# Row groups of 1, 3, 4 and 8 row tiles instead of 4, 6 and 6, and another order of the opening

## The chip, the cores and the metric

The kernel runs on one core of one Trainium2 chip. The metric is the device time of one execution in microseconds. Before the change the median of three runs was 1383.23 us (1383.08 to 1383.5). The profile is of one further execution.

## The reference, cut to what matters

One decoder block works on 256 rows `x` of width 2048 and on one conditioning vector `c`. What the change touches is its first part:

```
c_act = silu(c)
mod = c_act @ w_ada + b_ada              # 6 vectors of 2048
sh1, sc1, g1, sh2, sc2, g2 = split(mod, 6)
h = rms_norm(x, norm_mix_g) * (1.0 + sc1) + sh1
proj = h @ w_in                          # 2048 -> 1024 u, 1024 q, 1024 k, 1024 v, 2048 ga, 2048 gb
```

After it come a state-space branch on `u`, attention on `q`, `k`, `v`, a gated merge of both, `w_out`, a second modulated norm, a squared-ReLU MLP and a final norm. Everything is float32.

## The kernel before, in words

**The product.** `h` is held transposed, in 16 row tiles of 128 of the 2048 inner rows (`ah` is its high part, `al` the rest). A weight tile is 128 rows by 1024 columns, 512 KB. SP's queue loads it into one of 7 `wraw` buffers (`load`, L156). ScalarE casts its high part into one of 4 `whi` buffers (L161), VectorE subtracts to give the low part, one of 4 `wlo` buffers (L163). TensorE then does three products for each output piece: high by high, high by low, low by high. `gemm_t` does that with 24 matmuls of 256 columns for a tile (L208 to L210), `gemm_n` with 12 of 512 columns (L261 to L265). `whi` and `wlo` of a tile are free when TensorE has done with it, `wraw` when the low part is made.

**Row groups.** Row tile k of `h` needs entries of `sc1` and `sh1` that come from `w_ada`, 2 MB for each row tile. So the products with `w_in` are not run column block after column block over all 16 row tiles. `GR` cuts the row tiles into groups, and `qkvu(which, g0, g1)` runs one column block (0 q, 1 k, 2 v, 3 u, 4 the first half of ga) over the groups g0 to g1. `evac` (L1066) copies the four PSUM banks of the sums to SBUF. A later group of the same block starts from these sums: `seeded` (L192) copies them back into PSUM, and the first matmul waits for that. There are 5 banks for this, so four of a new product come free only as the last one's are copied out.

**w_ada.** Row tiles 0 to 3 take theirs on TensorE (`ada_first`): `wan` loads of 512 KB, four for each row tile (L283), 32 matmuls against the conditioning vector (L295, tile `adap`), a copy (L299), and a column of sums (L305, tile `adac`) that becomes `A1` and `B1` (L970, L971, L976). Row tiles 4 to 15 take theirs on VectorE (`ada_wide`): two row tiles need four tiles `ahm` of 128 by 2048, each of two 512 KB loads (L361) and one multiply-and-sum with `cb`, the vector silu(c) spread over all partitions (L367). The `ahm` buffers are four at first and two from the 13th load on; a load goes out when the sum that frees its buffer is done. After the fourth sum ScalarE makes two row tiles of `h` (`make_h1`, L500 and L161), and VectorE their low part (L163).

**Order.** Queues of jobs ("lanes") are advanced once for each weight tile, so a rate decides after how many tiles a `w_ada` sum or a piece of the state-space set-up is put in. `want` pulls the `w_ada` jobs forward if a tile would need a row tile that isn't yet made. The scheduler then orders each engine's instructions, and each engine and SP's queue work in that order.

**The opening.** `x` comes in four loads. ScalarE squares each (L477), VectorE adds halves (L478), TensorE sums over partitions (L480, tile `ss`). VectorE and ScalarE turn that into `R`, one over the root mean square (L483 to L488), `scale1` multiplies `x` by it (L493), `make_h1` applies `A1` and `B1`. `ada_bcast` (L413, L414) spreads silu(c) with 16 broadcast matmuls. `ssm_params` puts some 90 small operations on VectorE. `idle` (L130) issues matmuls whose result nobody reads, eight for each of row tiles 1 to 3.

Of the kernel before, what the change touches and what calls it, by code (L numbers as in the profile page):

```python
# [19 lines left out]
P = 128  # L20
S = 256
# [35 lines left out]
GR = (4, 6, 6)  # L57
# [20 lines left out]
class Kern:  # L78
    def __init__(self, ctx, tc, a, out):
# [15 lines left out]
        self.want = lambda kt: None  # L95

# [91 lines left out]

    def seeded(self, banks, seed):
        for o, d in zip(banks, seed or ()):  # L190
            with self.tc.high_priority(offset=OFF):
                self.nc.scalar.copy(*d(o))  # L192
        return bool(seed)

    def gemm_t(self, src, kts, c0, xh, xl, koff=0, mid={}, homes=(), seed=None):
# [4 lines left out]
        for i, (kt, hi, lo) in enumerate(self.stream(src, kts, c0, homes)):  # L200
# [39 lines left out]
    def gemm_n(self, src, kts, c0, xh, xl, koff=0, tail=1, mid={}, homes=(), seed=None):  # L240
# [5 lines left out]
        for i, unit in enumerate(self.stream(src, kts, c0, homes)):  # L246
# [158 lines left out]
    def ada_bcast(self, cols, dst, gate=None, turn=True):  # L405
        p = self.aux("adab")
        for i in range(4):
            with self.after(gate):
                o, c = p[:, i * P:(i + 1) * P], cols[:, i:i + 1].to_broadcast([P, P])
                if turn:  # L410
                    self.nc.tensor.transpose(o, c, self.ident)
                else:
                    self.nc.tensor.matmul(o, c, self.ident, start=True, stop=True)  # L413
# [57 lines left out]
    def norm1(self):  # L471
# [4 lines left out]
        for i in range(4):  # L476
            nc.scalar.activation(jk[:, i], x[:, 4 * i:4 * i + 4, :], AF.Square)  # L477
            v.tensor_add(jk[:, i, 0:2], jk[:, i, 0:2], jk[:, i, 2:4])  # L478
            for k in range(2):
                nc.tensor.matmul(p[:, 0:S], self.ones, jk[:, i, k], start=i + k == 0, stop=i + k == 4)  # L480
# [3 lines left out]
        nc.scalar.activation(s, w, AF.Sqrt)  # L484
# [5 lines left out]
    def scale1(self, k0, gate=None, n=2):  # L490
        x = self.x[:, k0:k0 + n, :]
        with self.after(gate):
            self.nc.vector.tensor_mul(x, x, self.R[:, None, :].to_broadcast([P, n, S]))  # L493
# [443 lines left out]
    def body(self):  # L937
        nc, a, v = self.nc, self.a, self.nc.vector
        with self.hot():
# [7 lines left out]
            v.memset(self.eps, EPS)  # L947
            nc.scalar.activation(self.col("dum0", 1), self.eps, AF.Silu)
# [7 lines left out]
            self.ident = self.col("ident", P)  # L956
            make_identity(nc, self.ident)
# [16 lines left out]
        def fin_shift(vec, B, k0, n):  # L974
            s = slice(k0, k0 + n)
            return lambda acc: v.tensor_add(B[:, s], acc, self.bada[vec][:, s])  # L976
# [561 lines left out]
```

## Time and profile before

| | |
|---|---|
| median of 3 runs | 1383.23 us |
| the profiled execution's own time | 1383.14 us |
| its span, first to last instruction | 1381.3 us |
| outside the span | 1.84 us |
| mean granted clock of TensorE | 0.996 |
| TensorE busy | 1352.4 us, 98% |
| VectorE busy | 1043.7 us, 76% |
| ScalarE busy | 741.1 us, 54% |

Times in the views are microseconds from the first instruction. A busy TensorE is not TensorE at its full rate: matmuls overlap, and the profile models their ends. The distance from one start to the next tells the rate.

### The profile page before, as it was taken

The page shows a single profiled execution, that of the slowest core. Times are in us where ns is not written, and L with a number is a line of the kernel's source. Part 1 is how long each engine was busy: PE and PEld are TensorE (multiplying, and loading weights), DVE is VectorE, ACT ScalarE, POOL GpSimd, SP SyncE. Part 2 cuts the span into 40 slices and gives each one's busy share as a digit, 9 for nine tenths or more (in the row PEclk, how much of TensorE's full clock was granted, in tenths as well). Part 3 has the DMA queues.
Part 4 walks back from the last instruction along what each step waited for, and adds up shares of the span by engine and source line. Part 5 has one row for each costly group of instructions (what it writes and reads, how often), then busy time and mean ns, then how long its engine had stood idle before and what let it go on. Part 6 is the DMA issues. An engine that isn't in the chain of part 4 may idle for free.

```text
span 1381.3 us, 21633 instructions
## 1 busy us (share of the span) xinstructions
PE 1352.4 (98%) x8338; PEld 1173.9 (85%) x8338; DVE 1043.7 (76%) x1449; ACT 741.1 (54%) x1020; POOL 42.6 (3%) x96
## 2 busy tenths in 40 slices
PE   6999999999999999999999999999999999999997
PEld 5888899988888887888999888888888888888885
DVE  6699987687898898988886976777666555555676
ACT  4466658656557643446565655444453554634543
POOL 1000000500003000000000000000000000000000
PEclk9999999999999999999999999999999999999999
DMA  9999965898447889898697878788878656566561
GB/s 371 387 400 371 354 206 176 263 333 280 164 160 235 298 294 341 294 391 290 212 361 242 284 248 251 244 251 286 246 240 242 200 189 197 188 190 195 179 202 64
DMA packets 112423, 356.43 MB, mean 258 GB/s; under 512 B 12240, under 2 KB 12272, under 8 KB 111904
## 3 DMA queue, kind: packets, MB, share of 16 engines
q1 hardware_dynamic: 109280, 348.96, 74.5%
q0 software_dynamic: 2896, 5.83, 1.4%
q8 instruction: 65, 1.06, 0.3%
q10 hardware_dynamic: 144, 0.26, 0.1%
q14 instruction: 38, 0.31, 0.1%
HBM read 350.79 MB, written 2.51 MB: 256 GB/s over the span
## 4 chain that ended last, share of the span: by engine, by line
PE 59%; DVE 3%; DMA 1%; ACT 1%; issue 1%; DVEq 0%; ACTq 0%
PE pd L226 13%; PE pn L261 11%; PE pn L263 11%; PE pn L265 11%; PE pd L230 7%; PE pt L208 2%; PE pt L210 2%; PE pt L209 2%; DVE wraw L325 1%; DMA wraw<-in_w_proj_ssm_dram 1%; DVE wlo L163 1%; DMA wraw<-in_w_out_dram 0%; DMA wraw<-in_w_ff_dram 0%; ACT whi L161 0%; PE trm L1232 0%
## 5 line engine op out<-in xcount | busy, mean ns | idle before, releaser
L161 ACT CAST whi<-wraw 128x1024 fp32r<-128x1024 f32 x448 | 467.6, 1051 | 516.7 <-PE pn L263 228.4
L163 DVE TENSOR_TENSOR wlo<-wraw,whi 128x1024 fp32r<-128x1024 f32 x448 | 545.2, 1223 | 253.4 <-ACT whi L161 248.5
L226 PE MATMUL pd<-h2h,whi 128*128 128x512 f32 x800 | 208.9, 393 | 0.0
L261 PE MATMUL pn<-whi,ff 128*128 128x512 f32 x496 | 193.0, 389 | 0.0
L263 PE MATMUL pn<-whi,ff 128*128 128x512 f32 x496 | 193.0, 389 | 0.0
L265 PE MATMUL pn<-wlo,ff 128*128 128x512 f32 x496 | 191.6, 389 | 0.0
L226 PEld LDWEIGHTS pd<-h2h,whi 128*128 128x128 f32 x800 | 140.5, 189 | 21.7
L325 DVE SCALAR_TENSOR_TENSOR wraw<-wraw,cb 128x1024 f32<-128x1024 f32 x128 | 156.2, 1221 | 0.0
L261 PE MATMUL pn<-whi,ah 128*128 128x512 f32 x320 | 126.3, 397 | 2.3 <-ACT ah L161 1.6
L230 PEld LDWEIGHTS pd<-h2h,wlo 128*128 128x128 f32 x800 | 116.1, 190 | 12.5
L263 PE MATMUL pn<-whi,ah 128*128 128x512 f32 x320 | 125.2, 391 | 0.0
L230 PE MATMUL pd<-h2h,wlo 128*128 128x256 f32 x800 | 119.3, 281 | 0.0
L265 PE MATMUL pn<-wlo,ah 128*128 128x512 f32 x320 | 115.1, 393 | 0.0
L208 PE MATMUL pt<-ah,whi 128*128 128x256 f32 x384 | 106.3, 287 | 6.4 <-ACT ah L161 4.7
L265 PEld LDWEIGHTS pn<-wlo,ff 128*128 128x128 f32 x496 | 93.1, 188 | 19.4
L261 PEld LDWEIGHTS pn<-whi,ff 128*128 128x128 f32 x496 | 93.1, 188 | 19.2
L263 PEld LDWEIGHTS pn<-whi,ff 128*128 128x128 f32 x496 | 93.1, 188 | 19.0
L209 PE MATMUL pt<-ah,whi 128*128 128x256 f32 x384 | 108.3, 287 | 0.0
L210 PE MATMUL pt<-ah,wlo 128*128 128x256 f32 x384 | 103.4, 285 | 0.0
L208 PEld LDWEIGHTS pt<-ah,whi 128*128 128x128 f32 x384 | 73.2, 194 | 7.6 <-ACT ah L161 5.4
L209 PEld LDWEIGHTS pt<-ah,whi 128*128 128x128 f32 x384 | 74.2, 193 | 1.3 <-issue 0.8
L261 PEld LDWEIGHTS pn<-whi,ah 128*128 128x128 f32 x320 | 60.0, 188 | 15.0 <-ACT ah L161 1.8
(378 smaller groups left out, 2016.8 us busy)
## 6 DMA issues: line engine op xcount, KB each, us to landing
wraw<-in_w_ff_dram SPq DMA_DIRECT2D x256, 512.0 KB, 4.8
wraw<-in_w_in_dram SPq DMA_DIRECT2D x128, 512.0 KB, 6.3
wraw<-in_wat_dram SPq DMA_DIRECT2D x128, 512.0 KB, 5.6
ahm<-in_wat_dram SPq DMA_DIRECT2D x48, 512.0 KB, 7.2
wraw<-in_w_out_dram SPq DMA_DIRECT2D x32, 512.0 KB, 6.4
wraw<-in_w_proj_attn_dram SPq DMA_DIRECT2D x16, 512.0 KB, 6.2
wraw<-in_w_proj_ssm_dram SPq DMA_DIRECT2D x16, 512.0 KB, 6.0
ahm<-in_wan_dram SPq DMA_DIRECT2D x8, 512.0 KB, 11.6
```

The costliest lines, as they stand in the source:

```text
L161: h = self.nc.scalar.copy(hi, src)
L163: s = self.nc.vector.tensor_sub(lo, src, hi.bitcast(F32))
L208: nc.tensor.matmul(o, hi[:, c], xh[:, kx, :], start=st, stop=False, skip_group_check=True)
L209: nc.tensor.matmul(o, hi[:, c], xl[:, kx, :], start=False, stop=False, skip_group_check=True)
L210: self.mm = nc.tensor.matmul(o, lo[:, c], xh[:, kx, :], start=False, stop=sp, skip_group_check=True)
L226: nc.tensor.matmul(banks[blk], hi[:, cut(blk, k)], x2[:, ks[k], :, :], start=i + k == 0, stop=False, skip_group_check=True)
L230: self.mm = nc.tensor.matmul(banks[blk][:, S:2 * S], lo[:, cut(blk, k)], x2[:, ks[k], 0, :], start=False, stop=last and k == 1, skip_group ...
L261: nc.tensor.matmul(o, xh[:, kx, tk], hi[:, c], start=q == 0 and not full, stop=False, skip_group_check=full)
L263: nc.tensor.matmul(o, xl[:, kx, tk], hi[:, c], start=False, stop=False, skip_group_check=full)
L265: self.mm = last = nc.tensor.matmul(o, xh[:, kx, tk], lo[:, c], start=False, stop=q == n - 1, skip_group_check=full)
L325: v.scalar_tensor_tensor(w, w, 1.0, self.cb[:, (i % 2) * 1024:(i % 2 + 1) * 1024], op0=OP.mult, op1=OP.mult, accum_out=pc[:, i:i + 1])
```

## The change

**Groups.** `GR` is (1, 3, 4, 8). The first group is one row tile, so q, k, v and u all take row tile 0 before row tile 1 is needed. The list of products has 17 entries instead of 13; 12 of them start from copied sums instead of 8. The last group has eight row tiles.

**Turns.** The `wan` loads of row tiles 1 to 3 are issued two at a time (`fetch`), with weights in between; the sums (`follow`) and the making of `h` (`finish`) are jobs of their own. `idle(8)` for row tiles 1 to 3 is gone. `ssm_params` is placed behind the first row tile of `h`. `scale1` of a row tile stands where its `h` is made.

**Opening.** Eight unread matmuls stand first on TensorE, three more behind each later pair of `ss`, six more before the first product. They use the tile of ones, not the weights. The identity is made at once, and the 16 broadcast matmuls of silu(c) stand ahead of the sums of squares, in four banks of the products' pool; their copies to `cb` are spread.

**Prime.** `prime` takes the first weight tile of the next product (load, cast, subtraction) ahead of the copies that end the one before; `flow` hands it on.

TensorE at the start of the program, before. `ss` is the sum of squares, `adap` and `adac` the sums of `w_ada`, `adab` the spread of silu(c), `pt` a bank of `gemm_t`:

```order
L480 MATMUL ss<-junk,s_69 128x256 x6
L295 MATMUL adap<-wraw,tz_70 32x128 x8
L480 MATMUL ss<-junk,s_69 128x256 x2
L295 MATMUL adap<-wraw,tz_70 32x128 x16
L413 MATMUL adab<-ident,tz_70 128x128 x8
L295 MATMUL adap<-wraw,tz_70 32x128 x8
L305 MATMUL adac<-s_69 128x1
L413 MATMUL adab<-ident,tz_70 128x128 x8
L305 MATMUL adac<-s_69 128x1
L208 MATMUL pt_341<-ah,whi 128x256
```

The same place with the change (three more rows of four broadcasts are left out):

```order
L131 MATMUL unread<-s_69 128x128 x8
L1022 MATMUL adab_126<-ident,tz_70 128x128 x4
...
L490 MATMUL ss<-junk,s_69 128x256 x4
L131 MATMUL unread<-s_69 128x128 x3
L490 MATMUL ss<-junk,s_69 128x256 x2
L131 MATMUL unread<-s_69 128x128 x3
L309 MATMUL adap<-wraw,tz_70 32x128 x6
L490 MATMUL ss<-junk,s_69 128x256 x2
L131 MATMUL unread<-s_69 128x128 x3
L309 MATMUL adap<-wraw,tz_70 32x128 x26
L319 MATMUL adac<-s_69 128x1 x2
L131 MATMUL unread<-s_69 128x128 x6
```

The whole spread and 14 unread matmuls now stand ahead of the last two sums of squares; before, those had eight `adap` ahead of them, and half of the spread stood between the last `adap` and the second `adac`.

SP's queue behind the loads of `x`, before (`wan` and `wat` are two layouts of `w_ada`; `ahm` and `ahs` are the buffers they land in): one weight tile stands behind the four loads of each row tile.

```order
L283 DMA wraw<-in_wan_dram 128x1024 x4
L156 DMA wraw<-in_w_in_dram 128x1024
L283 DMA ahm<-in_wan_dram 128x1024 x4
L156 DMA wraw<-in_w_in_dram 128x1024
L283 DMA ahm<-in_wan_dram 128x1024 x4
L156 DMA wraw<-in_w_in_dram 128x1024
L283 DMA ahs<-in_wan_dram 128x1024 x4
L156 DMA wraw<-in_w_in_dram 128x1024 x5
L361 DMA ahm<-in_wat_dram 128x1024 x4
```

With the change:

```order
L297 DMA wraw<-in_wan_dram 128x1024 x4
L157 DMA wraw<-in_w_in_dram 128x1024 x2
L297 DMA ahm<-in_wan_dram 128x1024 x2
L157 DMA wraw<-in_w_in_dram 128x1024
L297 DMA ahm<-in_wan_dram 128x1024 x2
L157 DMA wraw<-in_w_in_dram 128x1024
L297 DMA ahm<-in_wan_dram 128x1024 x2
L157 DMA wraw<-in_w_in_dram 128x1024
L297 DMA ahm<-in_wan_dram 128x1024 x2
L157 DMA wraw<-in_w_in_dram 128x1024 x2
L297 DMA ahs<-in_wan_dram 128x1024 x4
L157 DMA wraw<-in_w_in_dram 128x1024 x3
```

Seven weight tiles instead of three stand ahead of the last four `wan` loads. Counted along the whole queue, the order of weights and `w_ada` is the same again from about the 55th load on: in both kernels the last two loads for row tiles 14 and 15 are the 122nd and 123rd behind the conditioning vector, with 53 weight tiles ahead of them. But row tile 14 belongs to the 55th weight tile before the change and to the 47th with it.

VectorE at that place, with the change. `wlo_1902` is the low part of weight tile 46, `wlo_1921` of tile 47 (the first that needs row tile 14 of `h`), `wlo_1950`, `wlo_1970` and `wlo_2017` of tiles 48, 49 and 50; `ah_184<-htmp_1812` is the low part of row tiles 12 and 13, `ah_184<-htmp_1926` of 14 and 15:

```order
L164 TENSOR_TENSOR wlo_1902<-wraw_1899,whi_1901 128x1024
L164 TENSOR_TENSOR ah_184<-htmp_1812,ah_184 128x2x256
L381 SCALAR_TENSOR_TENSOR ahm_248,pw_276<-ahm_248,cb_104 128x2048
L164 TENSOR_TENSOR wlo_1921<-wraw_1918,whi_1920 128x1024
L984 TENSOR_TENSOR A1_122<-pw_276,cols_99 128x2
L985 SCALAR_TENSOR_TENSOR A1_122<-A1_122,cols_99 128x2
L381 SCALAR_TENSOR_TENSOR ahm_248,pw_277<-ahm_248,cb_104 128x2048
L164 TENSOR_TENSOR wlo_1950<-wraw_1947,whi_1949 128x1024
L381 SCALAR_TENSOR_TENSOR ahm_248,pw_277<-ahm_248,cb_104 128x2048
L164 TENSOR_TENSOR wlo_1970<-wraw_1967,whi_1969 128x1024
L164 TENSOR_TENSOR wlo_2017<-wraw_2014,whi_2016 128x1024
L992 TENSOR_TENSOR B1_123<-pw_277,cols_99 128x2
```

Before, `wlo_1934`, `wlo_1966` and `wlo_1998` are the low parts of weight tiles 48, 49 and 50, and row tile 14 is needed by tile 55:

```order
L367 SCALAR_TENSOR_TENSOR ahm_311,pw_340<-ahm_311,cb_95 128x2048
L163 TENSOR_TENSOR wlo_1934<-wraw_1931,whi_1933 128x1024
L163 TENSOR_TENSOR wlo_1966<-wraw_1963,whi_1965 128x1024
L663 TENSOR_TENSOR bp_1530<-tt_1101 128x32x16
L663 TENSOR_TENSOR tt_1101<-bp_1530,AB_285 128x512
L367 SCALAR_TENSOR_TENSOR ahm_311,pw_340<-ahm_311,cb_95 128x2048
L163 TENSOR_TENSOR wlo_1998<-wraw_1995,whi_1997 128x1024
```

So the last sum moves from behind tile 49 to behind tile 48, and the tile that needs it from 55 to 47. On ScalarE the cast of weight tile 50 stands ahead of the making of row tiles 14 and 15.

The diff, cut to its core:

```diff
-GR = (4, 6, 6)
+GR = (1, 3, 4, 8)
-    def idle(self, n):
-        o = self.aux("unread")[:, 0:S]
+    def idle(self, n, gate=None):
+        o = self.unread[:, 0:P]
         for _ in range(n):
-            with self.after(self.adac):
-                self.nc.tensor.matmul(o, self.whi[:, 0:P], self.whi[:, 0:S], start=True, stop=True)
+            with self.after(gate):
+                self.nc.tensor.matmul(o, self.ones, self.ones, start=True, stop=True)
+    def prime(self, *args):
+        gen = self.stream(*args)
+        self.primed = (next(gen), gen)
+
+    def flow(self, *args):
+        if self.primed:
+            first, gen = self.primed
+            self.primed = None
+            yield first
+        else:
+            gen = self.stream(*args)
+        yield from gen
...
+            if i:
+                self.idle(3, m)
...
+            self.unread = self.bank("unread")
+            self.idle(8)
+            self.ident = self.col("ident", P)
+            make_identity(nc, self.ident)
...
         with self.tc.high_priority(offset=OF1):
+            spread = [self.bank(f"adab{i}") for i in range(4)]
+            for k in range(KT):
+                nc.tensor.matmul(spread[k // 4][:, (k % 4) * P:(k % 4 + 1) * P], rc[:, k:k + 1].to_broadcast([P, P]),
+                                 self.ident, start=True, stop=True)
             self.norm1()
+            for i in range(4):
+                with self.after(self.root if i else None):
+                    nc.scalar.copy(self.cb[:, i * 512:(i + 1) * 512], spread[i])
...
-            self.scale1(0, n=1)
+            scaled = self.scale1(0, n=1)
+            self.idle(6, self.adac)
             self.make_h1(0, A1, B1, 1)
-            self.gates = [(None, self.acopy)]
-            for i in range(4):
-                self.ada_bcast(rc[:, 4 * i:4 * i + 4], self.cb[:, i * 512:(i + 1) * 512], turn=False)
-            self.ssm_params()
+            h0 = self.done[-1]
+            self.gates = [(scaled, self.acopy), h0]
...
-        self.lane("second", [follow(kt) for kt in (1, 2, 3)], 1.0)
+        self.lane("second", [scan_params, fetch(1, 0), both(fetch(1, 1), follow(1)),
+                              both(finish(1), fetch(2, 0)), both(fetch(2, 1), follow(2), finish(2)), nop,
+                              both(fetch(3, 0), fetch(3, 1), follow(3), finish(3))], 1.0)
...
-        for u in ((0, 0, 0), (1, 0, 0), (2, 0, 0), (3, 0, 0), (4, 0, 1), (3, 1, 1), (2, 1, 1), (1, 1, 1), (0, 1, 2),
-                  (4, 2, 2), (3, 2, 2)):
-            qkvu(*u)
-            if u == (4, 0, 1):
+        order = [(0, 0, 0), (1, 0, 0), (2, 0, 0), (3, 0, 0), (4, 0, 1), (3, 1, 1), (2, 1, 1), (1, 1, 1), (0, 1, 2),
+                 (1, 2, 2), (2, 2, 2), (3, 2, 2), (4, 2, 3), (0, 3, 3), (3, 3, 3)]
+        for u, after in zip(order, order[1:] + [None]):
+            qkvu(u, after)
+            if u == (0, 1, 2):
                 self.lanes["ssm"][1] = SR1
...
-        qkvu(1, 2, 2)
-        qkvu(2, 2, 2)
+        qkvu((1, 3, 3), (2, 3, 3))
+        qkvu((2, 3, 3))
```

More of the change, by code (lines that the diff above doesn't have):

```diff
@@ L403, in ringed, with ada_bcast @@
         return jobs
-    def ada_bcast(self, cols, dst, gate=None, turn=True):
+    def ada_bcast(self, cols, dst, gate=None):
         p = self.aux("adab")
@@ L408, in ada_bcast @@
             with self.after(gate):
[L409 to L413, printed above, removed]
+                self.nc.tensor.transpose(p[:, i * P:(i + 1) * P], cols[:, i:i + 1].to_broadcast([P, P]), self.ident)
         self.nc.scalar.copy(dst, p)
@@ L479, in norm1 @@
             for k in range(2):
-                nc.tensor.matmul(p[:, 0:S], self.ones, jk[:, i, k], start=i + k == 0, stop=i + k == 4)
+                m = nc.tensor.matmul(p[:, 0:S], self.ones, jk[:, i, k], start=i + k == 0, stop=i + k == 4)
+            if i:
+                self.idle(3, m)
         s = self.R = self.col("R", S)
@@ L1020, in body, with fetch, f @@
         homes = {1: regs[0:4], 2: regs[4:8], 3: [h[:, i, :] for h in h4 for i in range(2)]}
+        sums = {}
+        def fetch(kt, j):
+            def f():
+                with self.tc.high_priority(offset=OF1):
+                    if j == 0:
+                        sums[kt] = modn(kt, homes[kt])
+                    for ld, tot in sums[kt][j][0]:
+                        ld()
+            return f
         def follow(kt):
@@ L1024, in f, with finish, scan_params, both @@
                 with self.tc.high_priority(offset=OF1):
-                    parts = modn(kt, homes[kt], (self.mid, self.mm))
-                    for units, fold, last in parts:
+                    for units, fold, last in sums[kt]:
                         for ld, tot in units:
-                            ld()
-                    self.scale1(kt, n=1)
-                    totals(parts)
-                    self.idle(8)
+                            with self.after(self.mm):
+                                tot()
+            return f
+        def finish(kt):
+            def f():
+                with self.tc.high_priority(offset=OF1):
+                    for units, fold, last in sums[kt]:
+                        fold(self.mm)
+                    self.scale1(kt, self.done[-1][0], n=1)
                     self.make_h1(kt, A1, B1, 1)
-                    self.gates = [(None, self.acopy)] + ([(None, self.done[-1][1])] * 3 if kt == 3 else [])
             return f
+        def scan_params():
+            with self.after(h0[0]), self.after(h0[1]):
+                self.ssm_params()
+        def both(*fs):
+            return lambda: [f() for f in fs]
         self.early = False
@@ L1088, in body, with place, qkvu @@
                           + mod2(1) + mod2(2) + mod2(3))
-        def qkvu(which, g0, g1):
-            kts = range(groups[g0][0], sum(groups[g1]))
-            c0 = (1024, 2048, 3072, 0, 4096)[which]
+        def place(which, g0, g1):
+            return win, range(groups[g0][0], sum(groups[g1])), (1024, 2048, 3072, 0, 4096)[which]
+        def qkvu(u, after=None):
+            which, g0, g1 = u
             f = self.gemm_n if which in (2, 4) else self.gemm_t
-            evac(which, f(win, kts, c0, self.ah, self.al, seed=seeds(which) if g0 else None), g0)
+            banks = f(*place(*u), self.ah, self.al, seed=seeds(which) if g0 else None)
+            if after:
+                self.prime(*place(*after))
+            evac(which, banks, g0)
         ready = [0, 2]
```

15 lines of the change are left out of this document (8 added, 7 removed).

## The prediction

> **What bounds the kernel now.** I read the page first, for the engine that is always busy, then the chain of waits.
>
> ```profile
> PE 1352.4 (98%) x8338; PEld 1173.9 (85%) x8338; DVE 1043.7 (76%) x1449; ACT 741.1 (54%) x1020; POOL 42.6 (3%) x96
> PE 59%; DVE 3%; DMA 1%; ACT 1%; issue 1%; DVEq 0%; ACTq 0%
> ```
>
> TensorE sets the time, and the change takes no product away. So it can only save time in which TensorE stands still or runs slowly. The timeline of TensorE shows where that is, in the first 50 us:
>
> ```profile
> 6.65 5.26 PE L480 MATMUL ss<-junk,s 128*128 128x256 f32 x12 [6.65 <-DVE junk L478]
> 12.41 1.13 PE L480 MATMUL ss<-junk,s 128*128 128x256 f32 x4
> 14.49 2.05 PE L413 MATMUL adab<-ident,tz 128*128 128x128 f32 x16
> 22.77 1.22 PE L208 MATMUL pt<-ah,whi 128*128 128x256 f32 x4 [3.33 <-ACT ah L161]
> 24.00 0.41 PE L210 MATMUL pt<-ah,wlo 128*128 128x256 f32 x1
> 24.21 0.41 PE L208 MATMUL pt<-ah,whi 128*128 128x256 f32 x1
> 28.57 0.28 PE L209 MATMUL pt<-ah,whi 128*128 128x256 f32 x1
> 28.69 0.28 PE L210 MATMUL pt<-ah,wlo 128*128 128x256 f32 x1
> 29.50 1.08 PE L295 MATMUL adap<-ahm,tz 128*32 128x128 f32 x32
> 30.51 0.84 PE L305 MATMUL adac<-s 128*128 128x1 f32 x4
> 32.84 0.75 PE L208 MATMUL pt<-ah,whi 128*128 128x256 f32 x4 [0.45 <-ACT ah L161]
> 48.41 0.75 PE L208 MATMUL pt<-ah,whi 128*128 128x256 f32 x4 [0.45 <-ACT ah L161]
> ```
>
> The first product starts at 22.77 and runs at 0.21 us a matmul (24.00 to 24.21), later ones at 0.12. By 48.41 three weight tiles are done, 8.6 us of work. In between stand the sums of `w_ada` (2 x 1.08 a row tile), their columns, the unread matmuls. The view by windows, with the granted clock in the third column from the end, says the slow ones are the clock:
>
> ```profile
> 20.00:21.00 1.00, 0.00 (x0) 0.00 (x0) 1.00 (x5) 0.99 (x4) 0.00 (x0) 1.00 1.05 414
> 22.00:23.00 1.00, 0.23 (x1) 0.23 (x2) 0.93 (x7) 0.68 (x2) 0.00 (x0) 0.50 0.99 393
> 28.00:29.00 1.00, 1.00 (x7) 1.00 (x8) 0.00 (x0) 0.27 (x1) 0.00 (x0) 0.81 1.01 401
> 40.00:50.00 10.00, 9.04 (x113) 7.65 (x112) 3.94 (x8) 4.57 (x9) 0.51 (x1) 1.00 1.03 408
> ```
>
> The DMA share is about 1 all along, at 400 GB/s: 1.3 us for a 512 KB load.
>
> Behind 48 us TensorE hardly stops. The groups of 48.4 to 176 us:
>
> ```profile
> L208 PE MATMUL pt<-ah,whi 128*128 128x256 f32 x190 | 52.4, 284 | 2.2 <-ACT pt L192 1.7 <-ACT ah L161 0.4
> L261 PE MATMUL pn<-whi,ah 128*128 128x512 f32 x80 | 30.9, 393 | 1.6 <-ACT ah L161 1.6
> ```
>
> Each of the two lines is a third of its matmuls, so 23.7 tiles of 24 matmuls and 20 of 12: 43.7 tiles in 127.6 us, of which about 3.7 are the two stops named here. That is 2.84 us a tile, and three tiles before: 46.5 tiles are done at 175.5. This is the mark against which I set the change, since with it tile 47 is the first that needs row tile 14, and half a tile of the next product stands ahead of it.
>
> **The opening, step by step.** The last sum of squares comes at 13.4 now. With the change TensorE has ahead of its end 60 instructions of 128 columns (28 unread, 32 spread), 16 `ss` and 12 `adap`: at 0.12, 0.25 and 0.03 us (2.05/16, 1.13/4 less its tail, 1.08/32) 11.6 us from about 1.0 on, and 2 to 3 more while the clock is half. So it ends between 13.4 (the data themselves) and 15.6; I take 14.4. Starting early buys clock, not an earlier `R`. The steps behind it:
>
> ```profile
> 13.73 0.41 DVE L483 TENSOR_SCALAR tz<-ss 128x256 f32<-128x256 f32 x1
> 14.18 0.42 ACT L484 ACTIVATE R<-tz 128x256 f32<-128x256 f32 x1 [2.15 <-DVE tz L483]
> 14.69 1.75 DVE L485 RECIPROCAL R<-R 128x256 f32<-128x256 f32 x1
> 18.56 1.42 DVE L493 TENSOR_TENSOR xt<-xt,R 128x256 f32<-128x256 f32 x4
> 20.26 1.22 DVE L163 TENSOR_TENSOR wlo<-wraw,whi 128x1024 fp32r<-128x1024 f32 x1
> 21.68 0.60 ACT L500 ACTIVATE htmp<-xt,B,A 128x256 f32<-128x256 f32 x1 [0.50 <-DVE B L976]
> 22.31 0.40 ACT L161 CAST ah<-htmp 128x256 fp32r<-128x256 f32 x1
> ```
>
> Now the way from the last sum to the first product is 9.4 us, since parameter operations, four `scale1` and a low part stand between. With the change one `scale1` (0.36) is left and the low part stands behind: 0.4 + 0.4 + 1.75, four operations of 0.4, 0.4, A and B 0.3, 0.60 and 0.40, with gaps 6.4 us. The first product starts at 20.8, 2 us sooner and at full clock.
>
> From there TensorE takes 7 tiles (19.9), three pairs of `adap` (6.5), three `adac` (1.6), half a tile ahead of row tile 3 (1.4), and two waits: 1.5 for row tile 2, as 30.51 + 0.84 to 32.84 shows for such a step, and 2.5 for row tile 3, whose A1 stands behind a 2.2 us `w_ada` sum on VectorE. So tile 8 starts at 54 with 7.5 tiles done, where now there are 3 at 48.41 and 5 at 54. The loads allow it: the last `wan` load of row tile 3 is the 27th, 1.3 us each, about 38, nine before its use. The eight unread matmuls a row tile (1.2 each) go.
>
> **The middle.** 39 more tiles at 2.84 bring TensorE to tile 47 at 164.8: without a wait, 10.7 us ahead of the mark. What is late next is row tile 14. Views: VectorE's groups of 55.3 to 180 us, the tile `ahm`, and the timeline of VectorE, ScalarE and SP.
>
> ```profile
> L367 DVE SCALAR_TENSOR_TENSOR ahm<-ahm,cb 128x2048 f32<-128x2048 f32 x24 | 54.8, 2285 | 1.4 <-DMA ahm<-in_wat_dram 1.4
> L163 DVE TENSOR_TENSOR wlo<-wraw,whi 128x1024 fp32r<-128x1024 f32 x42 | 50.5, 1219 | 4.1 <-ACT whi L161 4.1
> L367 DVE SCALAR_TENSOR_TENSOR ahm<-ahm,cb x24: 2281/2284/2295, 55.4 to 177.8; 128x2048 f32<-128x2048 f32 x24
> DMA to landing us min/median/max: 4.5/7.2/10.3
> 55.38 2.28 DVE L367 SCALAR_TENSOR_TENSOR ahm<-ahm,cb 128x2048 f32<-128x2048 f32 x1
> 57.59 1.22 DVE L163 TENSOR_TENSOR wlo<-wraw,whi 128x1024 fp32r<-128x1024 f32 x1
> 58.72 2.28 DVE L367 SCALAR_TENSOR_TENSOR ahm<-ahm,cb 128x2048 f32<-128x2048 f32 x1
> 107.35 1.06 ACT L161 CAST whi<-wraw 128x1024 fp32r<-128x1024 f32 x1 [1.66 <-PE pn L263]
> 108.30 1.09 ACT L500 ACTIVATE htmp<-xt,B,A 128x256 f32<-128x256 f32 x2
> 109.42 0.62 ACT L161 CAST ah<-htmp 128x512 fp32r<-128x512 f32 x1
> 110.10 1.20 PE L261 MATMUL pn<-whi,ah 128*128 128x512 f32 x4 [1.65 <-ACT ah L161]
> ```
>
> VectorE's 24 sums advance 2.21 us each, a low part 1.14. Between the first and the end of the last stand, with the change, 24 sums, 38 low parts of weights, and 13 us of others (four `scale1`, six low parts of `h`, ten pieces of set-up, each 0.6): 109 us. Started at 51, behind `adac` of row tile 3, that ends at 160 if it never waits; TensorE's own way comes to 165. So the two are close, and a chain of buffers decides. Tile 46's cast needs the buffer of tile 42, done at 152.5. Then: cast 1.05, two row tiles made 1.1 and 0.6, low part 0.6, the sum that frees the buffer 2.2, SP's issue 0.5, the load 5.5, the last sum 2.2, two low parts 2.3, B 0.1, row tiles 14 and 15 made 1.1 and 0.6: 17.8 us. SP's queue is not in the way: the 53 weight tiles ahead of that load have their buffers by then. TensorE has 12.3 us of work in that time, so it waits 5.5. For the load I chose 5.5, between the least of the row (4.5) and its median (7.2), which comes from a fuller queue; the wait is 4.5 to 7.2 by these. With 0.5 lost on the way tile 47 starts at 170.8.
>
> Behind that, VectorE's low part of tile 51 stands behind eight set-up operations of 0.6, and TensorE waits about 1.0. The extra copies of four more products (16 out, 16 in, some 0.6 each) lie on ScalarE, 54% busy; they cost nothing where they run under the last product, and up to a stop like this one where they don't:
>
> ```profile
> 151.96 0.38 PE L208 MATMUL pt<-ah,whi 128*128 128x256 f32 x1 [1.71 <-ACT pt L192]
> ```
>
> Prime takes the first weight tile off these places; I count it 0, cover 1.1 us of cast. Sum: 175.5 - 170.8 - 1.0 = 3.7 us. The profiled execution took 1383.14, so **1379.4 us**; its time is 0.1 from the median shown. Behind 180 us everything shifts alike.
>
> **A rule against it.** The Trainium skill, page "TensorE: Matmul & The Clock Gate", section "🔬 Part 1: The HAM clock gate (the "warmup" mystery)", says that the clock falls after an idle window of some 3.4 us. By it the 1.4 us that I leave idle ahead of the first product are safe. The rows differ: the clock was still 1.00 in 20 to 21 and 0.50 in 22 to 23, so it fell some 2 us into a pause that began at 19.4.
>
> The Trainium skill, page "DMA: Bandwidth & Descriptors", section "Where 436 GB/s comes from", has HBM bind a core's loads at about 358 GB/s. The rows have up to 414. By the rule the 123 loads up to row tile 15's would land at about 182, and the rest of the chain (6.3 us) would put tile 47 at 188: 1396 us. By the rows they land at about 162, so this gets 0.01.
>
> **Rivals.**
> *VectorE and the loads keep pace.* Row tiles 14 and 15 are made before TensorE comes, at 165.3. For it: VectorE's sum ends at 160; against it, the buffers above. 175.5 - 165.3 - 1.0 = 9.2: 1373.9.
> *The clock falls in the pause.* The first tile and its sums then run at half rate as now, about 2.5 us: 1381.9.
> *Given back at the starts.* Two of the four added starts stop like 151.96 (1.87 with its own step): 1383.1. For it, one of eight did so now; against, these copies mostly run under the last product.
> *The sums keep their old pace.* Now they take 124.6 us from 55.38 to 180.0 (177.8, the last start, and 2.2), held by buffers, low parts and set-up. At that pace from 51 they end at 175.6, and with two low parts, B and the making of row tiles 14 and 15 (4.1) tile 47 starts at 179.7, 4.2 behind the mark: 1387.3, slower. It decides from 120 us on. Against it: its waits are for ScalarE's casts (4.1), that is for TensorE, which comes sooner.
>
> **How the numbers follow.** Chances: the forecast 0.45, keeping pace 0.22, clock 0.08, given back 0.12, old pace 0.12, the rule 0.01. The forecast's own range is 1376.5 to 1382, from the load (1 to 2 us) and the first product (1 either way). The range 1373.0 to 1384.5 leaves out the old pace and a little below. No change is within 0.2%, 2.8 us, about what a measurement can tell: 1380.4 to 1385.9. Faster takes 0.37 of the forecast, keeping pace and 0.02 of the clock: 0.61. No change is 0.08, 0.06 and 0.11 of given back: 0.25. The rest, 0.14, is slower.
>
> **What would show it.** The first product at 20 to 21.5 and 0.12 us apart; clock 1.00 from 8 us on. Tile 8 at 53 to 55. A wait of TensorE for `ah` of 4 to 7 us near 165 to 170, with VectorE's last sum at 166 to 168; no wait means keeping pace, a last sum behind 172 the old pace. It is wrong if TensorE waits for loads before 55, or if the starts from copied sums stop it by more than 2 us in all.

## The result: 9 us slower

| | before | changed |
|---|---|---|
| median | 1383.37 us (1383.08 to 1383.7, 4 runs) | 1392.57 us (1390.74 to 1393.36, 4 runs) |
| profiled execution | 1383.14 us | 1392.3 us |
| its span | 1381.3 us | 1390.5 us |
| ratio, 95% interval | | 1.0065 [1.0047, 1.0082] |

1379.4 was forecast, with a range up to 1384.5. From the first line of the page and the chain of waits of the changed kernel one sees only that TensorE still sets the time, and that VectorE and transfers now hold 5% each of the chain. (The shares of this chain add to 98%, those of the chain before to 65%, so they can't be set side by side.)

```profile
PE 1359.6 (98%) x8360; PEld 1180.9 (85%) x8360; DVE 1046.1 (75%) x1449; ACT 758.7 (55%) x1052; POOL 42.5 (3%) x96
PE 85%; DVE 5%; DMA 5%; ACT 2%; issue 1%; DVEq 0%; ACTq 0%; SPq 0%
```

The timeline of TensorE says where. These are the first product, the first use of row tile 3, the last matmul ahead of the long stop and the one behind it, and the first use of row tile 14 (tile 47):

```profile
20.45 0.73 PE L222 MATMUL pt<-ah,whi 128*128 128x256 f32 x4 [1.12 <-ACT ah L162]
21.13 0.28 PE L224 MATMUL pt<-ah,wlo 128*128 128x256 f32 x1
21.25 0.28 PE L222 MATMUL pt<-ah,whi 128*128 128x256 f32 x1
...
54.74 2.07 PE L275 MATMUL pn<-whi,ah 128*128 128x512 f32 x4 [3.41 <-ACT ah L162]
56.82 0.63 PE L277 MATMUL pn<-whi,ah 128*128 128x512 f32 x1
57.25 0.63 PE L279 MATMUL pn<-wlo,ah 128*128 128x512 f32 x1
...
170.21 0.28 PE L223 MATMUL pt<-ah,whi 128*128 128x256 f32 x1
176.67 0.58 PE L224 MATMUL pt<-ah,wlo 128*128 128x256 f32 x1 [6.18 <-DVE wlo L164]
...
179.71 2.08 PE L275 MATMUL pn<-whi,ah 128*128 128x512 f32 x4 [0.54 <-ACT ah L162]
```

The first product starts at 20.45 and goes at 0.12 us a matmul, as forecast. TensorE reaches row tile 3 on time, but behind the stop of 3.4 us its matmuls of 512 columns are 0.43 us apart (56.82 to 57.25) instead of 0.227. The windows of the changed kernel show the granted clock in the third column from the end:

```profile
53.00:54.00 1.00, 0.00 (x0) 0.00 (x0) 1.00 (x4) 0.35 (x1) 0.00 (x0) 1.00 1.02 375
54.00:55.00 1.00, 0.26 (x1) 0.27 (x2) 0.97 (x2) 0.65 (x2) 0.00 (x0) 0.51 1.05 420
60.00:61.00 1.00, 1.00 (x7) 0.90 (x6) 0.00 (x0) 1.00 (x3) 0.00 (x0) 0.58 1.00 401
173.00:174.00 1.00, 0.00 (x0) 0.00 (x0) 0.83 (x1) 0.00 (x0) 0.00 (x0) 0.74 0.79 262
183.00:184.00 1.00, 1.00 (x5) 0.76 (x4) 0.93 (x3) 0.00 (x0) 0.00 (x0) 0.64 0.00 0
```

A mean of 0.51 in a window that begins at full clock and ends at half puts the fall at 54.02; the others give a rise at 60.84, a second fall at 173.48 and a rise at 183.72. So each of the two stops is followed by work at half rate, some 6 to 7 us long, that is 3 us lost. There is a third fall far behind them. TensorE stops three times for ScalarE's work in the attention jobs, at 346.8, 348.1 and 349.8, for 0.46, 0.78 and 1.27 us. The row behind the last stop, and the clock there:

```profile
351.03 0.79 PE L275 MATMUL pn<-whi,ah 128*128 128x512 f32 x1 [1.27 <-ACT ga L1236]
```

```profile
350.00:351.00 1.00, 0.00 (x0) 0.00 (x0) 0.00 (x0) 1.00 (x3) 0.00 (x0) 0.99 0.00 0
354.00:355.00 1.00, 1.00 (x5) 0.77 (x5) 0.38 (x1) 0.99 (x2) 0.00 (x0) 0.80 0.00 0
```

That is a fall at 350.98 and a rise at 354.40: 3.4 us at half rate, 1.7 us lost.

The long stop is VectorE's. Its timeline in the changed kernel, from the low part of row tiles 12 and 13 to the operation that makes `B` of row tiles 14 and 15, with the last sum but two of `w_ada` at 163.30, and SP's issue of the last load:

```profile
162.70 0.68 DVE L164 TENSOR_TENSOR ah<-htmp,ah 128x512 fp32r<-128x512 f32 x1
163.30 2.28 DVE L381 SCALAR_TENSOR_TENSOR ahm<-ahm,cb 128x2048 f32<-128x2048 f32 x1
...
173.17 2.29 DVE L381 SCALAR_TENSOR_TENSOR ahm<-ahm,cb 128x2048 f32<-128x2048 f32 x1 [1.62 <-DMA ahm<-in_wat_dram]
175.39 2.36 DVE L164 TENSOR_TENSOR wlo<-wraw,whi 128x1024 fp32r<-128x1024 f32 x2
177.66 0.15 DVE L992 TENSOR_TENSOR B<-pw,cols 128x2 f32<-128x2 f32 x1
```

```profile
165.62 1.01 SPq L375 DMA_DIRECT2D ahm<-in_wat_dram  x2
```

The sum at 163.30 frees the buffer, SP issues the load at 165.62, the last sum can start at 173.17, and the low part for which TensorE stands still comes behind it, at 175.39. It is the low part of a weight tile of the next product; row tile 14 itself then comes only 0.54 us later. This is the chain that the prediction had.

### The profile page after: what moved, and what is told of

Read it like the earlier page. It is cut to its first block, busy times and chain, and to the rows that moved or that the text cites. A ratio compares the mean times of both kernels' runs of the same rounds, so it can differ in the third digit from the quotient of the medians.

```text
span 1390.5 us, 21699 instructions
## 1 busy us (share of the span) xinstructions
PE 1359.6 (98%) x8360; PEld 1180.9 (85%) x8360; DVE 1046.1 (75%) x1449; ACT 758.7 (55%) x1052; POOL 42.5 (3%) x96
## 4 chain that ended last, share of the span: by engine, by line
PE 85%; DVE 5%; DMA 5%; ACT 2%; issue 1%; DVEq 0%; ACTq 0%; SPq 0%
PE pn L275 15%; PE pn L277 15%; PE pn L279 15%; PE pd L240 13%; PE pd L244 7%; PE pt L224 5%; PE pt L222 5%; PE pt L223 5%; DVE wlo L164 2%; DMA ahm<-in_wat_dram 1%; DMA wraw<-in_w_in_dram 1%; DMA wraw<-in_w_proj_ssm_dram 1%; ACT whi L162 1%; DMA ct<-in_ct_dram 1%; PE rk L746 1%
## 5 line engine op out<-in xcount | busy, mean ns | idle before, releaser
L275 PE MATMUL pn<-whi,ah 128*128 128x512 f32 x320 | 127.0, 404 | 6.7 <-ACT ah L162 5.4
L277 PE MATMUL pn<-whi,ah 128*128 128x512 f32 x320 | 127.3, 398 | 0.0
L224 PEld LDWEIGHTS pt<-ah,wlo 128*128 128x128 f32 x384 | 71.4, 193 | 9.5 <-DVE wlo L164 9.3
L222 PEld LDWEIGHTS pt<-ah,whi 128*128 128x128 f32 x384 | 73.7, 193 | 2.8 <-ACT ah L162 1.3
```

The costliest lines, as they stand in the source:

```text
L222: nc.tensor.matmul(o, hi[:, c], xh[:, kx, :], start=st, stop=False, skip_group_check=True)
L224: self.mm = nc.tensor.matmul(o, lo[:, c], xh[:, kx, :], start=False, stop=sp, skip_group_check=True)
L275: nc.tensor.matmul(o, xh[:, kx, tk], hi[:, c], start=q == 0 and not full, stop=False, skip_group_check=full)
L277: nc.tensor.matmul(o, xl[:, kx, tk], hi[:, c], start=False, stop=False, skip_group_check=full)
```

## The experiments

The comparison of the traces leaves four things open: whether the half clock behind the stops counts, whether the sums follow TensorE or go at a pace of their own, what sets the last sum, and what the opening is worth by itself. Each kernel is the changed one with one edit, unless the text says otherwise. All compute the whole output.

The table has medians, the ratio with its interval to runs of the kernel before that were taken beside each kernel (their medians are 1382.88 to 1383.66), and three times of each profiled execution: the start of the first product; the time by which 46.5 weight tiles of the products are done, found by counting matmuls (24 of 256 columns or 12 of 512 for a tile; 175.45 in the kernel before); and what is left from there to the end of that execution's own time.

| kernel | median us | ratio, 95% interval | first product | 46.5 tiles | rest |
|---|---|---|---|---|---|
| before | 1383.37 | | 22.77 | 175.45 | 1207.7 |
| changed | 1392.57 | 1.0065 [1.0047, 1.0082] | 20.45 | 178.75 | 1213.6 |
| 48 unread at row tile 14 | 1394.21 | 1.0076 [1.0061, 1.0091] | 20.87 | 183.62 | 1211.5 |
| 26 unread at row tile 3 | 1392.53 | 1.0065 [1.0050, 1.0080] | 19.51 | 177.30 | 1212.8 |
| 14 and 24 unread | 1391.25 | 1.0059 [1.0041, 1.0078] | 20.68 | 176.33 | 1214.3 |
| first sum behind row tile 3 | 1388.60 | 1.0041 [1.0027, 1.0055] | 20.57 | 174.51 | 1214.1 |
| no unread matmuls | 1396.07 | 1.0094 [1.0074, 1.0114] | 19.46 | 182.31 | 1216.5 |
| old opening, new groups | 1394.96 | 1.0087 [1.0069, 1.0105] | 22.86 | 180.86 | 1215.4 |
| groups 1, 3, 6, 6 | 1387.46 | 1.0031 [1.0018, 1.0044] | 20.73 | 179.87 | 1207.2 |
| rate 0.70 | 1392.19 | 1.0066 [1.0048, 1.0084] | 19.51 | 176.09 | 1213.7 |
| set-up late | 1386.09 | 1.0015 [1.0006, 1.0025] | 19.57 | 174.90 | 1207.8 |
| set-up late, four buffers | 1389.49 | 1.0043 [1.0026, 1.0060] | 19.96 | 178.36 | 1211.1 |
| late, four buffers, 0.70, first sum behind row tile 3 | 1377.94 | 0.9954 [0.9939, 0.9969] | 20.76 | 169.25 | 1209.6 |
| the same with two buffers | 1378.02 | 0.9967 [0.9955, 0.9980] | 20.66 | 171.78 | 1205.9 |

A profiled execution can lie up to 3.4 us from its kernel's median (1382.74 with the set-up late, the fastest of ten), so the last three columns say where time goes, and the medians how much. Runs of one kernel lie up to 4.4 us apart.

### Does the half clock count?

Unread matmuls in the long stop, then in the stop at row tile 3:

```diff
+            if len(kts) == 12 and unit[0] == 14:
+                fl = self.aux("fill")
+                for _ in range(48):
+                    with self.after(self.mm):
+                        nc.tensor.matmul(fl[:, 0:P], self.ident, self.ident, start=True, stop=True)
```

> The changed kernel, with 48 unread matmuls of the identity (0.112 us each, 5.4 us) put on TensorE behind the last matmul of row tile 13 in the product that takes row tiles 4 to 15, where TensorE stood still from 170.4 to 176.7. They don't bring row tile 14 any sooner. Theory A (the granted clock fell because TensorE stood still, and the work from 176.7 to 183.7 then ran at half rate): the stop shrinks to under 1 us, the clock stays 1.00, and 3.3 us are saved: 1389.3. Rival (the low clock there has another cause, or the half rate is hidden by what TensorE waits for next): no change, 1392.6.

> The changed kernel, with 26 unread matmuls of the identity (2.9 us) behind the last adac of row tile 3, in the stop from 51.3 to 54.7. Theory A: the clock stays 1.00 from 54 on and tile 8 and its followers run 2.6 to 3 us sooner by 62. If VectorE's sums of w_ada follow TensorE (they stand in VectorE's order between low parts of weight tiles, whose buffers TensorE frees), the last sum comes 2.6 to 3 us sooner too: 1389.8. Rival B (the sums go at the pace of their loads and buffers, whatever TensorE does): the last sum stays at 173, the stop at row tile 14 grows by 2.6 to 3 us, and the time stays 1392.6.

(The code is in `gemm_n`, ahead of the matmuls of that row tile. The second kernel has 26 of them, at `len(kts) == 4 and unit[0] == 3`, behind `self.adac`.) Neither gave what theory A asked for, and neither tested it well: I had priced a matmul at 0.112 us, but each is two instructions. The unread matmuls of the first and of the second kernel, in their timelines:

```profile
171.59 10.88 PE L267 MATMUL fill<-ident 128*128 128x128 f32 x96
```

```profile
49.34 6.05 PE L267 MATMUL fill<-ident 128*128 128x128 f32 x52
```

They overran the stops of 6.2 and 3.4 us. The size was then set right, both in one kernel:

> The changed kernel with unread matmuls in both stops, sized by what the two kernels before this one showed (0.224 us for each 128x128 matmul, since each is two instructions of 0.112): 14 of them (3.1 us) behind the last adac of row tile 3, 24 (5.4 us) behind row tile 13. Theory A (a stop of over 3 us lets the granted clock fall, and the work behind it pays): the clock is 1.00 at 54 to 62 and at 176 to 185, both stops end where they ended, the first place is worth 2 to 3 us, the second 3 to 3.9, and 5 to 6.5 us are saved: 1386 to 1387.5. Rival (the low clock costs nothing there, since the next wait takes it up): under 1 us at each place, 1391 or more.

TensorE's timeline of that kernel at the two places, and its clock in two windows:

```profile
50.51 3.37 PE L269 MATMUL fill<-ident 128*128 128x128 f32 x28
55.02 1.20 PE L282 MATMUL pn<-whi,ah 128*128 128x512 f32 x4 [0.67 <-ACT ah L162]
...
167.79 5.52 PE L269 MATMUL fill<-ident 128*128 128x128 f32 x48
174.74 0.39 PE L224 MATMUL pt<-ah,wlo 128*128 128x256 f32 x1 [1.19 <-DVE wlo L164]
177.78 1.20 PE L282 MATMUL pn<-whi,ah 128*128 128x512 f32 x4 [1.17 <-ACT ah L162]
185.08 0.39 PE L224 MATMUL pt<-ah,wlo 128*128 128x256 f32 x1 [1.33 <-DVE wlo L164]
```

```profile
54.00:58.00 4.00, 3.33 (x17) 2.63 (x16) 3.90 (x6) 2.11 (x5) 0.00 (x0) 1.00 1.03 405
180.00:184.00 4.00, 3.75 (x18) 2.96 (x16) 3.90 (x7) 3.36 (x6) 0.00 (x0) 1.00 0.00 0
```

The clock stays at 1.00 at both places: that it fell for the stops is shown. It doesn't fall near 350 either. What it is worth differs. At row tile 3 the filled kernel is 2.4 us ahead by 46.5 tiles (176.33 against 178.75). Behind that nothing is won: the rest is 1214.3, no less than 1213.6 with half clock. TensorE at full rate runs into VectorE, which is late by then: 1.17 us for `ah`, 1.33 us at 185.08 for a low part. VectorE's timeline of the same kernel has, between the low part of row tiles 14 and 15 at 177.76 and that low part at 183.81, eight set-up operations, the first and last of which are

```profile
178.37 0.68 DVE L683 TENSOR_TENSOR tt<-cmp,AB 128x512 f32<-128x512 f32 x1
...
183.20 0.69 DVE L683 TENSOR_TENSOR bp<-tt 128x512 f32<-128x512 f32 x1
183.81 1.22 DVE L164 TENSOR_TENSOR wlo<-wraw,whi 128x1024 fp32r<-128x1024 f32 x1
```

So by these traces theory A holds at the first stop, and its rival at the second. The medians differ by 1.3 us, where 5 to 6.5 were expected, and the runs overlap (1389.96 to 1392.24 against 1390.74 to 1393.36). That the first stop's 2.4 us and nothing of the second count therefore rests on one trace of each kernel.

The clock's falls have a pattern. The Trainium skill, page "TensorE: Matmul & The Clock Gate", section "🔬 Part 1: The HAM clock gate (the "warmup" mystery)", says that the monitor looks at free-running windows of 3413 ns. The trace agrees closely: the changed kernel's half clock lasts 6.82 and 10.24 us, two and three times 3.41, and from the rise at 60.84 to the next fall at 173.48 are 112.64 us, 33.0 times 3.413. The third fall, at 350.98, is 167.26 us behind the rise at 183.72, 49.0 times.

In these traces every stop of TensorE of 2.1 us or more was followed by matmuls at half clock. The shortest of them is in the kernel with the rate of 0.70:

```profile
133.85 0.48 PE L224 MATMUL pt<-ah,wlo 128*128 128x256 f32 x1 [2.12 <-DVE wlo L164]
```

Of shorter stops some were and some weren't. The kernel with both stops filled has the same three stops in the attention jobs (0.46, 0.78 and 1.27 us) as the changed kernel, and its clock stayed up:

```profile
348.81 0.50 PE L282 MATMUL pn<-whi,ah 128*128 128x512 f32 x1 [1.27 <-ACT ga L1243]
```

```profile
348.00:352.00 4.00, 3.19 (x16) 2.63 (x16) 1.15 (x2) 3.98 (x9) 0.00 (x0) 1.00 0.00 0
```

That it depends on where in a step of 3.41 us such stops lie would fit; no run shows it.

### What makes the stop at row tile 3, and do the sums follow?

The sum at 51.19 stands on VectorE between the two operations that make `A1` of row tile 3. It was held behind the low part of that row tile:

```diff
                     self.make_h1(kt, A1, B1, 1)
+                    self.h3 = self.done[-1][0]
...
-            with self.after(self.done[-1][0]):
+            with self.after(self.h3 if k0 == 4 and vec == 1 and i == 0 else self.done[-1][0]):
                 sm = v.scalar_tensor_tensor(w, w, 1.0, self.cb, ...
```

> The changed kernel with VectorE's first w_ada sum for row tile 4 held behind the low part of row tile 3 of h; it stood between the two operations that make A1 of row tile 3. Theory D (that 2.2 us sum makes the stop of 3.6 us at row tile 3): the stop shrinks to 1.4 us, the clock stays 1.00 there, TensorE is 4 to 5 us earlier at 62, the sums follow it, the stop at row tile 14 stays at 6.3, and the time is 1388 to 1389. Rival B (the sums lose the 2.2 us and the stop at row tile 14 takes back what was saved): 1391.5 or more.

TensorE's timeline of that kernel, at row tile 3 and at the long stop:

```profile
52.72 1.20 PE L275 MATMUL pn<-whi,ah 128*128 128x512 f32 x4 [1.25 <-ACT ah L162]
...
172.42 0.58 PE L224 MATMUL pt<-ah,wlo 128*128 128x256 f32 x1 [6.04 <-DVE wlo L164]
```

As theory D said: the stop falls to 1.25 us, the long stop is as long as before (6.04 and 6.18) but 4.25 us earlier, and 4.0 us are saved in the median. The sums follow TensorE. The tile `ahm` in the changed kernel, and in this one:

```profile
L381 DVE SCALAR_TENSOR_TENSOR ahm<-ahm,cb x24: 2280/2284/2295, 51.2 to 173.2; 128x2048 f32<-128x2048 f32 x24
```

```profile
L381 DVE SCALAR_TENSOR_TENSOR ahm<-ahm,cb x24: 2279/2284/2293, 53.0 to 168.9; 128x2048 f32<-128x2048 f32 x24
```

They start 1.8 us later and end 4.3 us sooner: 115.9 us from first to last start instead of 122.0. So they keep no pace of their own. The other traces agree: in the seven kernels that have the changed kernel's order of sums and set-up, from the changed one to the one with the old opening, tile 42 is done at 154.9 to 162.8 (counted as for the table), and the last sum starts 13.8 to 14.6 us behind that in all of them.

### The opening and the groups apart

```diff
-            self.idle(8)
-            if i:
-                self.idle(3, m)
-            self.idle(6, self.adac)
```

> The changed kernel without its unread matmuls (8 at the start, 9 behind the sums of squares, 6 ahead of the first product); all else is left. Theory E (they buy clock for the first product): the first product runs at 0.21 us a matmul, and by the end of the first three tiles TensorE is 2 to 3 us later: 1394.5. Rival F (they stand ahead of the last sum of squares, which is bound by TensorE, and put off R): the sum of squares ends at about 13.5 instead of 14.7, the first product starts 1 us or more sooner, and what the clock costs is about made up: 1391 to 1393.

Both theories had a half. The timeline of the kernel without unread matmuls:

```profile
12.57 1.13 PE L490 MATMUL ss<-junk,s 128*128 128x256 f32 x4
...
19.46 1.22 PE L222 MATMUL pt<-ah,whi 128*128 128x256 f32 x4 [2.57 <-ACT ah L162]
20.48 0.41 PE L223 MATMUL pt<-ah,whi 128*128 128x256 f32 x1
20.69 0.41 PE L224 MATMUL pt<-ah,wlo 128*128 128x256 f32 x1
```

The last sum of squares ends 1 us sooner and the first product starts 1 us sooner, but at 0.21 us a matmul; the sum is 3.5 us slower. The unread matmuls are worth their place.

Next, the kernel before with `GR = (1, 3, 4, 8)` and the new order of products, and nothing else of the change (the place at which the set-up's rate drops goes with the order):

> The kernel before with the change's row groups and order of products alone: its own opening, turns and starts of products, without prime. Theory C (the groups make the stop at row tile 14: the sums follow TensorE by their places in VectorE's order, 46, 47 and 48 as with the whole change): a stop of 6 to 7 us near 172 to 179 with half clock behind it, the two stops of the kernel before at 108 and 150 gone, 1390 to 1395. Rival B (the sums end near 180 as in the kernel before, whatever the order): a stop of 9 us or more, 1396 or more. Rival (the stop at row tile 14 comes from the new opening's load order): no stop, 1380.

Its timeline has the same stop:

```profile
178.78 0.58 PE L210 MATMUL pt<-ah,wlo 128*128 128x256 f32 x1 [6.21 <-DVE wlo L163]
```

So the groups make the stop, whatever the opening, and cost some 11 us alone (1394.96 against 1383.66 beside it). The rest of the change gives about 2.4 us back.

### What sets the last sum?

Three edits at three places: the groups (row tile 14 needed by tile 55 again), the rate of the `w_ada` jobs, and then the buffers.

```diff
-GR = (1, 3, 4, 8)
+GR = (1, 3, 6, 6)
```

> The changed kernel with row groups of 1, 3, 6, 6 instead of 1, 3, 4, 8: row tile 14 is first needed by weight tile 55 as in the kernel before, instead of by tile 47, and row tiles 8 and 9 by tile 25 instead of 41. Theory C: no stop at row tile 14, and no half clock behind it: 10.4 us saved, 1382.2, and 1 to 2 us more if row tile 8 makes TensorE wait as it did before the change (1.8 us at 108). Rival B: the sums are late for an earlier row tile too, a stop of 4 us or more at row tiles 6 to 10, over 1387.

```diff
-R2 = .56
+R2 = .7
```

> The changed kernel with the rate of the w_ada jobs behind row tile 8 raised from 0.56 to 0.70 for each weight tile. In VectorE's order the last sum then stands behind the low part of weight tile 44 instead of 48, nothing else is meant to change. Theory C (the places in the order set the sums, and so the stop at row tile 14): the last sum starts at 162 to 166 instead of 173.2, the stop shrinks from 6.3 to under 1.5 us, the clock stays up, and 8 to 10 us are saved: 1383 to 1385. Rival B (the two buffers and their loads, some 7 us from a free buffer to the next sum, are at their limit already): the last sum comes less than 3 us sooner, VectorE waits for the loads instead, 1389 or more.

With groups of six the stop at row tile 14 is gone, and two others are there, both in the first tile that uses row tile 8. TensorE's timeline of that kernel:

```profile
110.84 0.73 PE L222 MATMUL pt<-ah,whi 128*128 128x256 f32 x4 [3.14 <-ACT ah L162]
113.07 0.58 PE L224 MATMUL pt<-ah,wlo 128*128 128x256 f32 x1 [1.49 <-DVE wlo L164]
```

5.1 us are saved, half of what theory C asked for; the sums are now late for an earlier row tile, as rival B said, for 4.6 us in two stops. With the higher rate the last sum starts at 166.5 instead of 173.2 and the long stop is gone, but stops in 121 to 134 (2.12 us at 133.85 and two under 1 us) and a rest that is no shorter leave nothing in the median. That suggests that the jobs were at the right place and VectorE had no time for them there. Part of what it does there is the state-space set-up. In the next kernel four of its operations (2.7 us) instead of ten (6.8 us) stand between 104 us and the last sum:

```diff
-SR1 = .27
+SR1 = .1
```

> A control for the two kernels behind it: the changed kernel with the rate of the state-space set-up during the row tiles 6 to 15 lowered from 0.27 to 0.10 jobs for each weight tile, so that the slot of two ahm buffers isn't asked for before row tile 14 is made. VectorE has some eight set-up operations of 0.6 us less ahead of the last sum. Theory C (loads and buffers and the places in the order make the stop at row tile 14): the stop stays at 6 to 6.5 us, 1391.5 to 1393. Rival G (VectorE's own work makes it): the stop falls by 2 us or more.

This was meant as a control, and it took 6.5 us off. The long stop is 3.69 us, and the rest is 1207.8 like that of the kernel before. From its timeline:

```profile
172.81 0.58 PE L224 MATMUL pt<-ah,wlo 128*128 128x256 f32 x1 [3.69 <-DVE wlo L164]
```

Half clock follows this stop too (matmuls of 256 columns took 0.41 us from 173.62 on), so it doesn't by itself make the rest of 1213.6 in the changed kernel. The three stops at 346.8 to 351.0 of the changed kernel and the fall of the clock behind them are gone. In the changed kernel TensorE has only the attention's matmuls from 345.2 to 351.0; here matmuls of a product stand between them. But this execution is the fastest of ten, 3.4 us under the median, so how much of that holds for a middle run isn't shown. Nor is it the set-up's place alone: the kernel with groups of six, with its set-up at the old rate, has a rest of 1207.2. Then the buffers:

```diff
-        ring = wide * 3 + wide[2:4] * 6
+        ring = wide * 6
-        free.update({i: (i + 4,) for i in range(8)})
-        free.update({i: (i + 2,) for i in range(10, 22)})
+        free.update({i: (i + 4,) for i in range(20)})
-            self.drain(5)
+            self.drain(8)
```

> As the kernel before this one, and all 24 w_ada sums use four ahm buffers; with the change the last 12 have two. The rates are left; the last four sums stand behind the low parts of weight tiles 43, 45, 46 and 47 instead of 46, 46, 47 and 48. Theory H (the stop at row tile 14 is the chain sum, freed buffer, load of 7.2 us, last sum): no wait of VectorE for these loads (2.7 us in the last two sums with the change), the last load goes out 5 us or more earlier, and the stop falls from 6.3 to 2 to 4 us: 1387 to 1390. Rival G (VectorE's own work and the place in the order): under 1 us is saved, 1391.5 or more. Rival (the DMA engines have no more to give): the last load lands within 2 us of where it did.

VectorE waits for no load any more, and the stop stays (4.0 us for the low part); the median is 3.4 us worse than with the late set-up alone. 1389.49 lies in the range of theory H only because the late set-up is in this kernel. The loads did make VectorE wait, but its order set the last sum. All together, and then the same with two buffers:

> The four buffers with the rate of the sums behind row tile 8 at 0.70 instead of 0.56 (the last sum behind the low part of weight tile 44), and the first sum held behind row tile 3 of h, which took 4.0 us off the median alone. Theory H: the loads land at 162 or sooner (123 of them at 1.29 us), the stop at row tile 14 is 0 to 2 us, the clock stays up, nothing is given back behind it but the 1 to 2 us near 346, and the time is 1377 to 1381, under the kernel before. Rival B (the sums and low parts fill VectorE: other stops of 2 us and more in 100 to 165 take the gain, as with the rate of 0.70 alone): 1385 or more.

> The last kernel (1377.9) with the last 12 sums in two ahm buffers again, as in the change; the rate of 0.70, the late set-up and the first sum behind row tile 3 stay. Theory H (at this rate the sums need the four buffers): VectorE waits 3 us or more for loads of w_ada between 110 and 165, TensorE has stops of 3 us or more there, 1381 to 1384. Rival G (the places in VectorE's order alone make the stop, the buffers nothing, as they did nothing at the rate of 0.56): 1377 to 1379.5.

1377.94 and 1378.02. The long stop is gone in both. The late set-up saved 6.5 us by itself and the held-back sum 4.0; the three edits together save 14.6. So the rate, which gained nothing alone, seems to be worth some 4 us beside them; no kernel has the other two without it. In the second, VectorE's idle time until a load landed (us, times), from the view of the tile `ahm`, and its longest stop of TensorE between 104 and 182:

```profile
  DMA ahm<-in_wat_dram: 5.1, 6
```

```profile
130.42 0.39 PE L224 MATMUL pt<-ah,wlo 128*128 128x256 f32 x1 [1.06 <-DVE wlo L164]
```

VectorE waits 5.1 us for loads and TensorE hardly feels it, so rival G holds: the buffers add nothing here, and what counted were the places of the sums and of the set-up in VectorE's order. Both kernels beat the one before the change, by 0.46% and 0.33%.

## Why the prediction was wrong, by its own steps

**The first product** (20.8 forecast, 20.45 measured) and **tile 8** (54, and 54.74) were right. The wait for row tile 3 was 2.5 forecast and 3.41 measured, behind the sum that the step named; it didn't ask for the granted clock behind it.

**TensorE's way to tile 47: the step that failed first.** "39 more tiles at 2.84 bring TensorE to tile 47 at 164.8" took full rate from 54 on; TensorE stood at the stop at 170.2 with half a tile still to do ahead of it, and tile 42, from which the chain starts, was done 6.0 us late (below). Half rate from 54.74 to 60.84 took 3.05 us of them, the later start of tile 8 0.7, and four waits for low parts, a row of the changed kernel's view of waits for 62 to 165,

```profile
PE pt L224 <- DVE wlo L164: 1.8, 4, 1.1
```

1.8: together 5.6. The forecast had stops of 2.5 and 5.5 us and priced them at their own length; what the clock would do behind them it asked only for the pause of 1.4 us ahead of the first product.

**The chain to tile 47** was the right mechanism, with terms too small. It was to start when tile 42 is done and end 17.8 us later. ScalarE's timeline of the changed kernel has its cast for tile 46, released by TensorE, at

```profile
158.51 1.06 ACT L162 CAST whi<-wraw 128x1024 fp32r<-128x1024 f32 x1 [1.66 <-PE pn L277]
```

6.0 later than the 152.5 of the forecast, and to 179.71 are 21.2 us. From SP's issue to the last sum are 7.55, where 0.5 and 5.5 were taken: 1.55 of the 3.4 us. Another 1.4 lie ahead of that: from the cast to the sum at 163.30 are 4.79 us, where 3.35 was taken, since a set-up operation and a low part of weights (at 160.96 and 161.56) stand ahead of the low part of row tiles 12 and 13 on VectorE. Tile 47 came 8.9 us late. The wait itself (4.5 to 7.2 forecast) was 6.18 for a low part and 0.54 for `ah`; since the chain starts from TensorE, time lost upstream goes through it unshortened, as the kernel with the first sum held back shows from the other side.

**Behind tile 47** 1.0 us was forecast, and 5.0 came: 9.2 in all (1392.3 - 1383.14) less the 4.2 by which tile 47 is behind the mark of 175.5. The traces name these: half rate from 179.71 to 183.72 (2.0 us), the three stops in the attention jobs (2.5) and the half rate behind them (1.7). That is 6.2 us, more than the difference; the kernel before has a stop of 0.64 us in the same jobs too. The prediction priced one wait behind tile 47, and none of these. 8.9 and 4.0 are the 12.9 us between 1379.4 and 1392.3.

**The rivals.** "The sums keep their old pace" gave tile 47 at 179.7, and 179.71 was measured; the end of the last sum at 175.6, and it was 175.4. That was luck, and its reason was wrong: the sums keep no pace, they followed TensorE. It was right by two losses that it didn't know. Its sum also left out the 1.0 us behind tile 47 that the others took; with it, it gives 1388.3. "Given back at the starts" and "the clock falls in the pause" did not happen. The rule told in the prediction from the Trainium skill, page "DMA: Bandwidth & Descriptors", section "Where 436 GB/s comes from", that HBM binds a core's loads at some 358 GB/s, did not show: the windows at 53 to 61 have 375 to 420.

**The opening** was judged right in sign, and too large. Its 2.3 us at the first product are about the 2.4 that the medians show for all of the change but the groups; that they are the same us isn't shown. Nothing of the 10.7 us that TensorE was to be ahead of the mark was left at tile 47, which came 4.2 behind it.

Open is why the groups of eight with the set-up in its place cost time far behind it, in the attention jobs: the traces show where, but why the attention's matmuls bunch there was not followed.

## What to carry to other kernels

If work is moved so that a late input is needed sooner, follow the input's whole chain on the engine that makes it, and ask what stands ahead of it in that engine's order; here part of a set-up that nobody waited for could go behind it, and with it a rate that gained nothing alone may have become worth its place. Price a stop of TensorE with the clock behind it, and then ask whether anything else is late by then: by the traces the same 3 us counted at one stop and not at the other. A loss upstream of a chain that starts from the bound engine comes out at its end in full.

## What was not expected of the hardware

The granted clock falls and rises on a grid. In the changed kernel the changes at 54.02, 60.84, 173.48, 183.72 and 350.98 lie 2, 33, 3 and 49 steps of 3.41 us apart. In the opening, kernels with the same instructions differ. The 16 broadcasts of silu(c), two instructions each, in the kernel with groups of six and in the one with the rate of 0.70, whose openings are the same:

```profile
4.63 4.79 PE L1022 MATMUL adab<-ident,tz 128*128 128x128 f32 x32
```

```profile
4.47 3.74 PE L1022 MATMUL adab<-ident,tz 128*128 128x128 f32 x32
```

In the second the spread ran at full rate from its start and took 1.05 us less, so the clock came up earlier, and the first product starts at 19.51 instead of 20.73. That the same steps set this is likely, and not shown. The 20.45 of the changed kernel is one draw of these. TensorE has work without a pause from 1.05 us to the sums of squares now, so this goes into the time of `R`; over these openings the first product starts at 19.51 to 20.87.
